# A hybrid decoder step on one core: loads and sums of the output projection in another order, more projection passes ahead of three places, the first memory-output products by heads, one table load per norm

## The chip, the cores and the metric

One core of a Trainium2 chip runs the whole step in one launch. The metric is the device time in microseconds (us). Before the change three runs gave 2590.53, 2591.98 and 2594.45 us, median 2591.98.

## What is computed

One decoder layer over 512 prompt tokens and 8 x 4 sample tokens (544 columns in all, width 2048): a mixer of two head groups, attention over a small memory, and a SwiGLU block, each behind an RMSNorm, in fp32.

```python
def decoder_layer(x, ...):
    y, ... = token_mixer(rmsnorm(x, norm_mix_w), ...)   # h @ w_in; 8 HGRN2 heads and 16 window heads; concat @ w_out
    x = x + y
    x = x + memory_attend(rmsnorm(x, norm_xattn_w), ...)  # q = h @ w_mq, softmax(q k) v, @ w_mo
    x = x + swiglu(rmsnorm(x, norm_ffn_w), ...)           # (silu(h @ w_gate) * (h @ w_up)) @ w_down
    return x, ...
...
def hgrn2_scan(q, k, g, v, s0):   # S_t = diag(exp g_t) S_{t-1} + k_t v_t^T, o_t = S_t^T q_t
```

## The kernel before, in words

All activations are held transposed, features on 128 partitions and tokens along the free dimension. A weight or an operand is split in two parts, hi (ScalarE, ACT) and lo (VectorE, DVE: the value minus hi); a product is three matmul passes, hi·hi, hi·lo, lo·hi, accumulated in PSUM. TensorE (PE) runs these passes from 60 us to the end, almost without a break. A tile framework schedules the program and fixes the order of instructions on each engine; each engine, and the queue of each engine that issues DMAs, works through its own list in order.

**HGRN heads** (250 to 790 us, `hgrn_head`, L910). Head h needs a chain of eight levels: PE forms `ha_ps` (L933) of qp and kp, DVE multiplies qp (L953) and kp (L956) by decays, and the next level's matmuls need these. Between the levels `draw(n)` (L355) takes n steps from the line of waiting matmul work, projection passes `in_ps` (L345) most of the time, so that PE has something to do. Ahead of level 0 stands `draw(8)` (L920). While head 0 runs, DVE and POOL (GpSimd) also prepare the window attention of the samples (`qbd` L771 and L786). While head 7 runs, the first unit of the output projection is being prepared already.

**Output projection** (786 to 974 us, `out_unit`, L1083). Eight units: two halves of the mixer's rows (r1 first, then r2) times four blocks of 512 output columns, in the order r1-0, r1-2, r1-3, r1-1, r2-2, r2-3, r2-0, r2-1. A unit multiplies a 1024 x 512 block of weights by a Strassen-like scheme in seven products, in the order B11, B21, T2, T1, T3, B22, T4. It loads four quarters A11, A21, A12, A22 (`oraw`, 512 KB each, issued on the SP queue, L1093). POOL forms S1 = A21 + A22, S2 = S1 - A11, S3 = A21 - A11 and later U = A12 - S2 (`ocomb`, L1099). The products take as weights, in their order: A11, A12, S2, S1, S3, U, A22. Each is split on ACT (`ohi` L1136, half by half `oh` L1137) and DVE (`olo` L1138) ahead of its 24 matmuls (`o_ps`, L1150); DVE adds the sums to x (L611). The operands B and T of a row group are made by `Rows` (L630 to L647): POOL forms sums of mixer outputs (`ot` L634, `mix` L635, L645, L647), ACT and DVE split them (`oB`, `oT`, L606 and L607). For r2 this work hangs in unit r1-1 as its hook: `rows2_parts` (L1241) is called after products 1 and 3. Units r2-3, r2-0 and r2-1 have a hook too, which splits and squares the finished rows of x for the next norm. For units r1-1 to r2-1 the quarter A22 comes from a pool wx with two buffers, the other three from a pool wr with four.

**Memory attention** (974 to 1076 us). `add_mq` (L1445) projects queries, `norm_rows` (L1232) makes 1/rms with Ln and Exp on ACT, one call of `rsqrt` (L80) per half of the columns, each with a load of the table set (L77). Then eight (head, half) units run: scores (`x_scores`, `xs_ps` L1465), softmax, transposes (`x_turn`, `xt_ps` L1476) and values (`x_values`, `xo_ps` L1487), with `draw` between them; the samples' part (`xso_ps` L1415, `xot_ps` L1425) is mixed in.

**Memory output** (1066 to 1140 us, `add_mo`, L1540). Product i takes the outputs of the four heads, `oxh`/`oxl`, as moving operand. The loop runs over the three passes outside and over the heads k inside, so that the last head is needed by the eighth matmul. `add_mo(0, 0)` and `add_mo(1, 0)` are queued right behind the last unit's values. After each product DVE adds to x (L1556) and, from the third on, ACT, DVE and POOL make the operands of the next block (`ffn_parts`, L1575).

**Feed-forward** (1136 to 2585 us): gate and up (`s_ps`, L1703; splits `shi` L1645, `h` L1646, `slo` L1647; POOL sums `scomb` L1665), then down. Their order is untouched but for the first gate unit, where the third `norm_rows` stands.

Of the kernel before, what the change touches and what calls it, by code (L numbers as in the profile page):

```python
# [19 lines left out]
P = 128  # L20
# [24 lines left out]
def hybrid_step(ctx: ExitStack, tc: tile.TileContext, a):  # L45
# [863 lines left out]
    def hgrn_head(h):  # L909
# [174 lines left out]
    def out_unit(rows, o4, old, hook=None):  # L1084

        n0 = o4 * 4 * P

        def load(f, c, last=False):
            p, n = (wx[0], 2) if rows2_on and last else (wr, 4)
            t = p.tile([P, WCH * P], F32, tag="raw", name="oraw", bufs=n)  # L1090
            t = t.rearrange("p (k c) -> p k c", k=DN)
            c0 = n0 + c * 2 * P
            dma(t, w_out[f * P : (f + DN) * P, c0 : c0 + 2 * P].rearrange("(k p) c -> p k c", p=P))  # L1093
            return t

        def comb(x, y, op):
            t = wst.tile([P, WCH * P], F32, tag="raw", name="ocomb", bufs=3)
            t = t.rearrange("p (k c) -> p k c", k=DN)
            nc.gpsimd.tensor_tensor(t, x, y, op)  # L1099
            return t  # L1100

        f0 = rows.g * 4
        A11, A21, A12, A22 = load(f0, 0), load(f0, 1), load(f0 + DN, 0), load(f0 + DN, 1, True)

        def run():
            S1 = comb(A21, A22, ALU.add)
            S2 = comb(S1, A11, SPLIT)
            S3 = comb(A21, A11, SPLIT)
            accs = [acc_tile("o_ps") for _ in range(2)]
            if next(units_made) % 2:  # L1110
                accs.reverse()
            o, x = (
                {
                    q: y[:, 2 * i : 2 * i + 2, t]
                    for q, (i, t) in dict(c11=(0, T0), c12=(0, T1), c21=(1, T0), c22=(1, T1)).items()
                }
                for y in (old, X[o4])
            )
            for i, (q, src, bank, first, dst, fresh) in enumerate((
                ("B11", A11, 0, True, "c11", True), ("B21", A12, 1, True, "c11", False),  # L1120
                ("T2", S2, 0, False, "c12", True), ("T1", S1, 1, True, "c22", True),
                ("T3", S3, 0, False, "c22", False), ("B22", None, 1, False, "c12", False),
                ("T4", A22, 0, False, "c21", True),
            )):
                rows.part(i)
                if src is None:
                    src = comb(A12, S2, SPLIT)
                hi = wst.tile([P, WCH * P], F32R, tag="hi", name="ohi")
                lo = wst.tile([P, WCH * P], F32R, tag="lo", name="olo")
                hi, lo = (t.rearrange("p (k c) -> p k c", k=DN) for t in (hi, lo))  # L1130
                if heads_done:
                    for j in range(2):
                        js = slice(2 * j, 2 * j + 2)
                        h2 = ps_to[0].tile([P, 2, 2 * P], F32R, tag="to"[j], name="oh2")
                        if j == 0:
                            nc.scalar.copy(hi, src)  # L1136
                        nc.scalar.copy(h2, src[:, js])  # L1137
                        nc.vector.tensor_tensor(lo[:, js], src[:, js], h2.bitcast(F32), SPLIT)  # L1138
                else:
                    split(hi, lo, src)  # L1140
                rows.part(i + 1)
                if hook:
                    hook(i)
                xh, xl = rows.ops[q]
                acc = accs[bank]
                for wt, xt_, at in ((hi, xh, 0), (hi, xl, 1), (lo, xh, 2)):
                    for p in range(2):
                        s = slice(p * P, (p + 1) * P)
# [78 lines left out]
    def norm_rows(out, sums, tag="t"):  # L1227

        for (b, e), s in zip(HALF, sums):
            pt = ps("nr_ps", tag)[:, : TT // 2]  # L1230
            n = s.shape[1]
            for u in range(n):  # L1232
                nc.tensor.matmul(pt, ones, s[:, u], start=u == 0, stop=u == n - 1)
            v = small.tile([P, TT], F32, tag="nv", name="nv", bufs=1)[:, : TT // 2]
            nc.vector.tensor_scalar(v, pt, 1.0 / D, EPS, ALU.mult, ALU.add)
            t = small.tile([P, TT], F32, tag="sqt", name="nt", bufs=2)[:, : TT // 2]
            rsqrt(out[:, b:e], v, t)

    rows2 = []

# [263 lines left out]
    for n, u in enumerate(units):  # L1504
        need(("mq", *u))
        if n:
            x_turn(*units[n - 1])
            draw(4)
        else:
            draw(36)  # L1510
        x_scores(*u)
        draw(14)
        if n:
            x_values(*units[n - 1])
        for _ in range(6 if n >= MH - 1 else 0):
            x_more(1)
            draw(5)
# [21 lines left out]
    def add_mo(i, half, done=None):  # L1539


        def run():
            if i not in mo_w:
                mo_w[i] = [next(wparts) for _ in range(MH)]
            acc = acc_tile("mo_ps")
            for at in range(3):
                for k, hi, lo in mo_w[i]:
                    wt, xt_ = (hi, hi, lo)[at], ox[half][k][at % 2]
                    for u in range(2):
                        nc.tensor.matmul(  # L1550
                            acc[:, u, :HT], wt[:, u * P : (u + 1) * P], xt_,
                            start=k + at == 0, stop=k == MH - 1 and at == 2,
                        )
                        yield
# [578 lines left out]
```

## Time and profile before

| | |
|---|---|
| median of three runs | 2591.98 us (2590.53 to 2594.45) |
| profiled execution | 2587.27 us, span 2585.5 us, mean granted clock 0.993 |
| PE busy | 2511.4 us, 97% of the span |
| DVE, ACT, POOL busy | 1708.9, 1557.7, 1104.3 us (66%, 60%, 43%) |
| DMA | 315.44 MB, 122 GB/s on average |

The profiled execution is the sum's base: 2587.27 us, of which 2585.5 are the span and 1.8 lie around it. It is 4.7 us under the median.

How to read it: PE is the engine that ends everything, so time is won or lost where PE waits. A row of PE's timeline shows in square brackets how long PE stood idle before the group and what ended that. PEclk in the windows view is the clock granted to TensorE as a share of 2.4 GHz (0.50 is 1.2 GHz).

### The profile page before, as it was taken

Reading aid. Unit: us, or ns where it says so; the run is one execution under the profiler, and the core shown is the slowest. Engines: PE = TensorE matmul, PEld = TensorE weight load, DVE = VectorE, ACT = ScalarE, POOL = GpSimd, SP = SyncE. Lnnn points to the kernel's source line nnn. Section 1 sums busy time; section 2 is a strip of 40 time slices with the busy share of each in tenths; the row PEclk is TensorE's granted clock in tenths of the full one; section 3 lists DMA queues with packets and bytes.
Section 4 is the critical chain, followed back from the end, with each engine's and each line's share of the span. In section 5 each row is a group of like instructions: output and inputs, shape, how many; then the busy total and the mean of one; then the engine's idle time right before and its main releaser. Section 6 shows DMA issues by size and latency. Waiting matters only on the chain.

```text
span 2585.5 us, 48037 instructions
## 1 busy us (share of the span) xinstructions
PE 2511.4 (97%) x19679; PEld 2443.3 (95%) x19679; DVE 1708.9 (66%) x2560; ACT 1557.7 (60%) x2181; POOL 1104.3 (43%) x643
## 2 busy tenths in 40 slices
PE   8999999999999999989999999999999999999997
PEld 7999999998998998779999999999999999999987
DVE  5555655565559796497666666666666676777887
ACT  5343223333327685467677777777776778767767
POOL 4101122122125631165555555555555566665752
PEclk9999999999999999999999999999999999999999
DMA  7222323554524226523333333333333453333325
GB/s 240 83 68 82 91 83 92 152 149 143 182 66 135 91 73 186 187 93 107 116 107 117 114 123 113 122 115 113 116 107 116 142 211 133 101 131 133 116 70 164
DMA packets 287164, 315.44 MB, mean 122 GB/s; under 512 B 9508, under 2 KB 239220, under 8 KB 284097
## 3 DMA queue, kind: packets, MB, share of 16 engines
q1 hardware_dynamic: 273024, 264.80, 32.2%
q0 software_dynamic: 13920, 47.58, 5.6%
q8 instruction: 155, 2.54, 0.4%
q14 instruction: 65, 0.52, 0.1%
HBM read 278.28 MB, written 33.64 MB: 121 GB/s over the span
## 4 chain that ended last, share of the span: by engine, by line
PE 54%; DVE 6%; ACT 3%; issue 2%; DMA 2%; POOL 1%; ACTq 0%; DVEq 0%; POOLq 0%; SPq 0%
PE s_ps L1703 48%; PE o_ps L1150 3%; PE d_ps L1987 1%; PE mq_ps L1445 1%; DVE slo L1647 1%; DMA wraw<-in_w_down_dram 1%; DVE wlo L132 1%; ACT shi L1645 0%; ACT h L1646 0%; DVE x L1887 0%; DMA xkv<-in_cache_mem_v_dram 0%; POOL scomb L1665 0%; DVE olo L1138 0%; DMA wraw<-in_w_mq_dram 0%; PE xk_ps L1363 0%
## 5 line engine op out<-in xcount | busy, mean ns | idle before, releaser
L1647 DVE TENSOR_TENSOR slo<-scomb,h 128x1024 fp32r<-128x1024 f32 x256 | 312.5, 1221 | 243.2 <-ACT h L1646 232.8
L1645 ACT CAST shi<-scomb 128x1024 fp32r<-128x1024 f32 x256 | 269.2, 1052 | 190.8 <-PE s_ps L1703 168.9
L131 ACT CAST whi<-wraw 128x1024 fp32r<-128x1024 f32 (+1 forms) x204 | 169.4, 845 | 342.0 <-PE in_ps L345 278.4
L1665 POOL TENSOR_TENSOR scomb<-sraw 128x1024 f32<-128x1024 f32 (+1 forms) x134 | 319.4, 2386 | 7.5 <-DVE slo L1647 2.5
L1665 POOL TENSOR_TENSOR scomb<-sraw,scomb 128x1024 f32<-128x1024 f32 (+1 forms) x67 | 166.5, 2486 | 327.9 <-DVE slo L1647 319.3
L1645 ACT CAST shi<-sraw 128x1024 fp32r<-128x1024 f32 x192 | 201.6, 1050 | 160.9 <-issue 99.5
L345 PE MATMUL in_ps<-xh,whi 128*128 128x272 f32 x1280 | 276.6, 297 | 0.8 <-ACT whi L131 0.8
L345 PE MATMUL in_ps<-xl,whi 128*128 128x272 f32 x1280 | 274.2, 295 | 0.0
L345 PE MATMUL in_ps<-xh,wlo 128*128 128x272 f32 x1280 | 272.1, 294 | 0.9 <-DVE wlo L132 0.8
L132 DVE TENSOR_TENSOR wlo<-wraw,whi 128x1024 fp32r<-128x1024 f32 (+1 forms) x204 | 208.0, 1033 | 96.6 <-ACT whi L131 92.1
L1646 ACT CAST h<-scomb 128x1024 fp32r<-128x1024 f32 x256 | 258.6, 1010 | 3.1 <-DVE slo L1647 3.0
L1647 DVE TENSOR_TENSOR slo<-sraw,h 128x1024 fp32r<-128x1024 f32 x192 | 233.8, 1218 | 28.0 <-ACT h L1646 23.2
L345 PEld LDWEIGHTS in_ps<-xh,whi 128*128 128x128 f32 x1280 | 201.8, 189 | 6.6 <-issue 4.3
L345 PEld LDWEIGHTS in_ps<-xh,wlo 128*128 128x128 f32 x1280 | 201.9, 189 | 6.4 <-issue 4.4
L345 PEld LDWEIGHTS in_ps<-xl,whi 128*128 128x128 f32 x1280 | 202.0, 189 | 5.1 <-issue 4.4
L1646 ACT CAST h<-sraw 128x1024 fp32r<-128x1024 f32 x192 | 194.1, 1011 | 17.8 <-DVE slo L1647 17.6
L1703 PE MATMUL s_ps<-T,shi 128*128 128x272 f32 x1408 | 191.9, 288 | 0.9 <-DVE T L607 0.5
L1703 PEld LDWEIGHTS s_ps<-T,shi 128*128 128x128 f32 x1408 | 182.8, 188 | 1.5 <-ACT T L606 0.8
L611 DVE TENSOR_TENSOR gu<-gu,s_ps 128x272 f32<-128x272 f32 x264 | 111.3, 435 | 109.4 <-PE s_ps L1703 106.8
L1703 PE MATMUL s_ps<-dT,shi 128*128 128x272 f32 x1280 | 173.8, 288 | 2.7 <-ACT h L1646 1.4
L1703 PEld LDWEIGHTS s_ps<-dT,shi 128*128 128x128 f32 x1280 | 165.1, 188 | 3.6 <-ACT h L1646 1.6
L1665 POOL TENSOR_TENSOR scomb<-scomb,sraw 128x1024 f32<-128x1024 f32 (+1 forms) x67 | 160.4, 2395 | 4.2
(523 smaller groups left out, 5723.6 us busy)
## 6 DMA issues: line engine op xcount, KB each, us to landing
sraw<-in_w_gate_dram SPq DMA_DIRECT2D x44, 1024.0 KB, 5.1
sraw<-in_w_up_dram SPq DMA_DIRECT2D x44, 1024.0 KB, 5.1
wraw<-in_w_in_dram SPq DMA_DIRECT2D x84, 512.0 KB, 4.0
sraw<-in_w_down_dram SPq DMA_DIRECT2D x40, 1024.0 KB, 5.2
oraw<-in_w_out_dram SPq DMA_DIRECT2D x32, 512.0 KB, 3.9
h_d<-gu POOLq DMA_DIRECT2D x22, 544.0 KB, 4.6
wraw<-in_w_mk_dram SPq DMA_DIRECT2D x16, 512.0 KB, 3.7
wraw<-in_w_mv_dram SPq DMA_DIRECT2D x16, 512.0 KB, 3.9
```

Source lines behind the costliest of these rows:

```text
L131: nc.scalar.copy(hi[:, s], raw[:, s])
L132: nc.vector.tensor_tensor(lo[:, s], raw[:, s], hi[:, s].bitcast(F32), SPLIT)
L345: nc.tensor.matmul(acc[:, i, : e - b], wt, xt[:, b:e], start=j + at == 0, stop=j == KD - 1 and at == 2,)
L611: nc.vector.tensor_tensor(out, x, y, ALU.add)
L1150: nc.tensor.matmul(acc[:, p, :HT], wt[:, k, s], xt_[:, k], start=first and k + at == 0, stop=k == DN - 1 and at == 2, skip_group_check=True,)
L1445: nc.tensor.matmul(acc, wt, xt_, start=j + at == 0, stop=j == KD - 1 and at == 2)
L1645: first = nc.scalar.copy(hi, src)
L1646: nc.scalar.copy(h2, src)
L1647: return first, nc.vector.tensor_tensor(lo, src, h2.bitcast(F32), SPLIT)
L1665: ins = nc.gpsimd.tensor_tensor(t[:, p], x[:, p], y[:, p], op)
L1703: nc.tensor.matmul(accs[p], wt[:, k, s], xt_[:, k], start=k + at == 0, stop=k == n - 1 and at == 2,)
L1987: nc.tensor.matmul(acc[:, 0, : e0 - b0], (hi, hi, lo)[at], hp[k][at % 2][:, b0:e0], start=k + at == 0, stop=k == nf - 1 and at == 2,)
```

## The change

Five edits. (1) In heads 0 and 7 the draw ahead of level 0 takes 16 steps instead of 8. (2) In units with a hook the loads are issued in the order A11, A21, A22, A12, all four from wr, and what the hook issues is ordered behind the unit's S3. (3) `norm_rows` loads the table set for the first half only. (4) The draw ahead of the first scores takes 47 steps instead of 36. (5) The first two memory-output products run head by head: all three passes of head 0, then of head 1, and so on.

```diff
@@ hgrn_head
-        draw(8)
+        draw(8 if 0 < h < H - 1 else 16)
@@ out_unit
             t = t.rearrange("p (k c) -> p k c", k=DN)
-            nc.gpsimd.tensor_tensor(t, x, y, op)
-            return t
+            return t, nc.gpsimd.tensor_tensor(t, x, y, op)
...
-        A11, A21, A12, A22 = load(f0, 0), load(f0, 1), load(f0 + DN, 0), load(f0 + DN, 1, True)
+        A11, A21 = load(f0, 0), load(f0, 1)
+        if hook:
+            A22 = load(f0 + DN, 1)
+            A12 = load(f0 + DN, 0)
+        else:
+            A12, A22 = load(f0 + DN, 0), load(f0 + DN, 1, True)
...
-            S3 = comb(A21, A11, SPLIT)
+            S3, summed = comb(A21, A11, SPLIT)
...
                 if hook:
-                    hook(i)
+                    with tc.issue_after(summed.ins):
+                        hook(i)
@@ norm_rows
-            rsqrt(out[:, b:e], v, t)
+            rsqrt(out[:, b:e], v, t, preload=b == 0)
@@ memory attention
-            draw(36)
+            draw(47)
@@ add_mo
-            for at in range(3):
-                for k, hi, lo in mo_w[i]:
-                    wt, xt_ = (hi, hi, lo)[at], ox[half][k][at % 2]
...
+            order = [(at, part) for at in range(3) for part in mo_w[i]]
+            if done is None and i < 2:
+                order.sort(key=lambda o: o[1][0])
+            for n, (at, (k, hi, lo)) in enumerate(order):
+                wt, xt_ = (hi, hi, lo)[at], ox[half][k][at % 2]
```

The numbers of instructions stay as they were, but for two table loads fewer on ACT. What moves shows at three places. (Line numbers of the changed kernel are up to seven higher.)

**The loads of unit r1-1 on the SP queue.** 9108, 9110, 9112 and 9114 are A11, A21 and the two others; the waits are semaphores of other engines and of DMA queues. Before:

```order
L1093 DMA oraw_9114<-in_w_out_dram 128x4x256 [waits DMASW5_49,DMASW4_49,DMASW6_49,DMASW2_49,DMASW7_49,DMASW1_49,DMAHW6_49,DVE_49,PE_49]
L1093 DMA oraw_9381<-in_w_out_dram 128x4x256
L1093 DMA oraw_8856<-in_w_out_dram 128x4x256 [waits DMAHW2_49,DVE_49]
L1093 DMA oraw_9108<-in_w_out_dram 128x4x256 [waits DMAHW3_49,DVE_49,Pool_49]
L1093 DMA oraw_9110<-in_w_out_dram 128x4x256 [waits DMAHW4_49]
L1093 DMA oraw_9112<-in_w_out_dram 128x4x256 [waits DMAHW5_49,Pool_49]
```

Now:

```order
L1093 DMA oraw_9381<-in_w_out_dram 128x4x256 [waits DMASW5_49,DMASW6_49,DMASW4_49,DMASW7_49,DMASW2_49,DMAHW6_49,DMASW1_49,PE_49]
L1093 DMA oraw_8856<-in_w_out_dram 128x4x256 [waits DMAHW2_49,DVE_49]
L1093 DMA oraw_9108<-in_w_out_dram 128x4x256 [waits DMAHW3_49,DVE_49,Pool_49]
L1093 DMA oraw_9110<-in_w_out_dram 128x4x256 [waits DMAHW4_49]
L1093 DMA oraw_9112<-in_w_out_dram 128x4x256 [waits DMAHW5_49,Pool_49]
L1093 DMA oraw_9114<-in_w_out_dram 128x4x256 [waits DMAHW1_49,Pool_49]
```

Before, 9114 is A22 and goes out ahead of the rest, and 9112 is A12. Now 9112 is A22 and 9114, the last, is A12, and 9114 waits for POOL: the program puts it into the buffer of 9110, this unit's A21, which S1 and S3 read. In r2-0 and r2-1 it is the same: the fourth load takes the buffer of the unit's own A21, the third that of the A12 that the unit before reads last in its U.

**POOL and ACT around unit r1-1.** 9036 is U of unit r1-3; 9116, 9118, 9120 and 9305 are S1, S2, S3 and U of r1-1. POOL now:

```order
L1099 TENSOR_TENSOR ocomb_9036<-oraw_8854,ocomb_8860 128x1024
L1099 TENSOR_TENSOR ocomb_9116<-oraw_9110,oraw_9112 128x1024
L1099 TENSOR_TENSOR ocomb_9118<-ocomb_9116,oraw_9108 128x1024
L1099 TENSOR_TENSOR ocomb_9120<-oraw_9110,oraw_9108 128x1024
L634 TENSOR_TENSOR ot1_9167<-mix0_406 128x1088
L635 TENSOR_TENSOR mix0_406<-mix0_406,mix1_407 128x4x272
L645 TENSOR_TENSOR mix0_406<-mix0_406 128x4x272
L647 TENSOR_TENSOR mix1_407<-mix1_407,mix0_406 128x4x272
L1099 TENSOR_TENSOR ocomb_9305<-oraw_9114,ocomb_9118 128x1024
```

ACT now, from B11's split (9124) to B21's (9158):

```order
L1141 CAST oh2_9126<-oraw_9108 128x512
L1140 CAST ohi_9124<-oraw_9108 128x1024
L1141 CAST oh2_9130<-oraw_9108 128x512
L606 CAST oT3_9508<-mix0_406 128x1088
L1141 CAST oh2_9160<-oraw_9114 128x512
L1140 CAST ohi_9158<-oraw_9114 128x1024
L1141 CAST oh2_9164<-oraw_9114 128x512
```

Before, L634, L635 and L645 stood on POOL ahead of the sums of unit r1-3, the unit before, and oT3's cast stood on ACT far ahead of r1-1; only L647 lay between S3 and U. Now all four lie between S3 and U, and oT3's cast, which reads what L635 writes, stands ahead of the cast of A12.

**PE at the end of the memory attention.** 10513, 10515, 10517 and 10519 are the hi parts of heads 0 to 3 (lo: one number higher). Before:

```order
L1550 MATMUL mo_ps<-oxh_10513,whi 128x272 x2
L1550 MATMUL mo_ps<-oxh_10515,whi 128x272 x2
L1550 MATMUL mo_ps<-oxh_10517,whi 128x272 x2
L1415 MATMUL xso_ps<-xkv,xpm 32x128 x8
L1425 MATMUL xot_ps<-ident,xos 128x128
L1476 MATMUL xt_ps<-ident,p 128x128 x4
L1487 MATMUL xo_ps<-pT,vm__10511 128x256 x2
L1550 MATMUL mo_ps<-oxh_10519,whi 128x272 x2
L1550 MATMUL mo_ps<-oxl_10514,whi 128x272 x2
```

Now, from xot on:

```order
L1430 MATMUL xot_ps<-ident,xos 128x128
L1557 MATMUL mo_ps<-oxh_10517,wlo 128x272 x2
L1557 MATMUL mo_ps<-oxh_10513,whi 128x272 x2
L1557 MATMUL mo_ps<-oxl_10514,whi 128x272 x2
L1557 MATMUL mo_ps<-oxh_10513,wlo 128x272 x2
L1557 MATMUL mo_ps<-oxh_10515,whi 128x272 x2
L1557 MATMUL mo_ps<-oxl_10516,whi 128x272 x2
L1557 MATMUL mo_ps<-oxh_10515,wlo 128x272 x2
L1557 MATMUL mo_ps<-oxh_10517,whi 128x272
L1481 MATMUL xt_ps<-ident,p 128x128 x4
L1557 MATMUL mo_ps<-oxh_10517,whi 128x272
L1557 MATMUL mo_ps<-oxl_10518,whi 128x272 x2
```

Ahead of the last head's values `xo_ps` stood 12 matmuls of the first two products before, and 36 of their 48 now; between `xot_ps` and `xt_ps` stood none, and 15 now; between `xt_ps` and `xo_ps` none, and 5 now.

## Rows read from the trace of the kernel before

**Rows 1.** the page, part 4: the chain that ended last, by engine

```profile
PE 54%; DVE 6%; ACT 3%; issue 2%; DMA 2%; POOL 1%; ACTq 0%; DVEq 0%; POOLq 0%; SPq 0%
```

**Rows 2.** waits view, PE: what for, us in total, times, longest

```profile
PE mo_ps L1550 <- DVE x L1556: 7.8, 5, 2.8
PE s_ps L1703 <- DVE slo L1647: 6.8, 7, 2.0
PE o_ps L1150 <- ACT ohi L1136: 3.7, 1, 3.7
PE ha_ps L933 <- DVE kp L956: 3.4, 2, 1.8
```

**Rows 3.** timeline, PE, 838 to 886: start, us, engine, line, operation

```profile
847.98 2.75 PE L1150 MATMUL o_ps<-oT,ohi 128*128 128x272 f32 x16 [3.69 <-ACT ohi L1136]
867.71 2.18 PE L1150 MATMUL o_ps<-oB,ohi 128*128 128x272 f32 x16
881.48 2.25 PE L1150 MATMUL o_ps<-oB,ohi 128*128 128x272 f32 x16 [1.53 <-DVE x L611]
```

**Rows 4.** timeline, POOL, 831 to 884

```profile
832.27 2.55 POOL L634 TENSOR_TENSOR ot<-mix 128x1088 f32<-128x1088 f32 x1
834.90 3.47 POOL L635 TENSOR_TENSOR mix<-mix,mix 128x1088 f32<-128x1088 f32 x1
841.96 2.47 POOL L1099 TENSOR_TENSOR ocomb<-oraw 128x1024 f32<-128x1024 f32 x1 [0.94 <-DMA oraw<-in_w_out_dram]
851.91 2.40 POOL L1099 TENSOR_TENSOR ocomb<-oraw,ocomb 128x1024 f32<-128x1024 f32 x1 [2.74 <-issue]
859.24 2.42 POOL L1099 TENSOR_TENSOR ocomb<-oraw 128x1024 f32<-128x1024 f32 x1
```

**Rows 5.** timeline, ACT, 832 to 885

```profile
866.30 0.59 ACT L1137 CAST oh<-ocomb 128x512 fp32r<-128x512 f32 x1 [0.82 <-DVE olo L1138]
866.96 1.05 ACT L1136 CAST ohi<-ocomb 128x1024 fp32r<-128x1024 f32 x1
868.43 1.10 ACT L606 CAST oB<-mix 128x1088 fp32r<-128x1088 f32 x1
```

**Rows 6.** DMA issues, windows 853 to 859 and 919 to 925: median us to landing last

```profile
oraw<-in_w_out_dram SPq DMA_DIRECT2D x1, 512.0 KB, 3.5
oraw<-in_w_out_dram SPq DMA_DIRECT2D x1, 512.0 KB, 3.9
```

**Rows 7.** windows view: us, busy times, PEclk, DMA share, GB/s

```profile
850.00:855.00 5.00, 5.00 (x31) 5.00 (x30) 3.69 (x6) 3.62 (x7) 3.01 (x2) 0.71 0.64 210
1074.00:1076.00 2.00, 1.57 (x4) 0.68 (x2) 0.00 (x0) 0.37 (x1) 0.00 (x0) 0.50 0.00 0
```

**Rows 8.** timeline, POOL then PE, 890 to 975

```profile
917.43 2.76 POOL L1099 TENSOR_TENSOR ocomb<-oraw,ocomb 128x1024 f32<-128x1024 f32 x1 [11.49 <-issue]
925.82 2.43 POOL L1099 TENSOR_TENSOR ocomb<-oraw 128x1024 f32<-128x1024 f32 x1
933.65 2.16 PE L1150 MATMUL o_ps<-oB,ohi 128*128 128x272 f32 x16
```

**Rows 9.** timeline, DVE then POOL, 750 to 790

```profile
755.79 2.59 DVE L956 TENSOR_TENSOR kp<-kp,tot 128x256 f32<-128x256 f32 x1
755.67 2.42 POOL L1099 TENSOR_TENSOR ocomb<-ocomb,oraw 128x1024 f32<-128x1024 f32 x1 [1.36 <-DVE wlo L132]
```

**Rows 10.** timeline, DVE, 248 to 272

```profile
258.78 2.67 DVE L786 COPY qbd<-sqs 64x64 f32<-64x64 f32 x2 [0.18 <-POOL qbd L771]
```

**Rows 11.** timeline, PE, 1050 to 1205

```profile
1071.68 1.09 PE L1476 MATMUL xt_ps<-ident,p 128*128 128x128 f32 x4 [1.92 <-DVE oxl L1339]
1076.03 0.82 PE L1550 MATMUL mo_ps<-oxh,whi 128*128 128x272 f32 x2 [0.46 <-ACT oxh L1338]
```

**Rows 12.** timeline, ACT, 982 to 996

```profile
984.82 1.28 ACT L77 ACT_TABLE_LOAD   x1
986.89 1.05 ACT L131 CAST whi<-wraw 128x1024 fp32r<-128x1024 f32 x1 [0.78 <-DMA wraw<-in_w_mq_dram]
```

More of the change, by code (lines that the diff above doesn't have):

```diff
@@ L1098, in comb @@
             t = t.rearrange("p (k c) -> p k c", k=DN)
-            nc.gpsimd.tensor_tensor(t, x, y, op)
-            return t
+            return t, nc.gpsimd.tensor_tensor(t, x, y, op)
         f0 = rows.g * 4
-        A11, A21, A12, A22 = load(f0, 0), load(f0, 1), load(f0 + DN, 0), load(f0 + DN, 1, True)
+        A11, A21 = load(f0, 0), load(f0, 1)
[4 more added lines that the diff above has]
+            A12, A22 = load(f0 + DN, 0), load(f0 + DN, 1, True)
         def run():
-            S1 = comb(A21, A22, ALU.add)
-            S2 = comb(S1, A11, SPLIT)
-            S3 = comb(A21, A11, SPLIT)
+            S1, _ = comb(A21, A22, ALU.add)
+            S2, _ = comb(S1, A11, SPLIT)
+            S3, summed = comb(A21, A11, SPLIT)
             accs = [acc_tile("o_ps") for _ in range(2)]
@@ L1126, in run @@
                 if src is None:
-                    src = comb(A12, S2, SPLIT)
+                    src, _ = comb(A12, S2, SPLIT)
                 hi = wst.tile([P, WCH * P], F32R, tag="hi", name="ohi")
@@ L1545, in run @@
             acc = acc_tile("mo_ps")
-            for at in range(3):
-                for k, hi, lo in mo_w[i]:
-                    wt, xt_ = (hi, hi, lo)[at], ox[half][k][at % 2]
[L1549 to L1554, printed above, removed]
+            order = [(at, part) for at in range(3) for part in mo_w[i]]
[3 more added lines that the diff above has]
+                wt, xt_ = (hi, hi, lo)[at], ox[half][k][at % 2]
+                for u in range(2):
+                    nc.tensor.matmul(
+                        acc[:, u, :HT], wt[:, u * P : (u + 1) * P], xt_,
+                        start=n == 0, stop=n == len(order) - 1,
+                    )
+                    yield
             x = X[i // 2][:, 2 * i % 4 : 2 * i % 4 + 2, (T0, T1)[half]]
```

## The prediction, made before the changed kernel ran

> **What bounds the kernel now.** I read the chain that ended last first: more than half of it is TensorE [rows 1], and PE is busy 97% of the span. So the change can only win or lose where PE stands still. Next I read the waits view for PE: its largest entries are a few microseconds in all and lie at the places that the diff touches [rows 2]. Then each place in the timelines: which wait ends last there, and what stands ahead of it on the engine that releases it. The granted clock comes last: after the 3.69 us wait of PE at 847.98 [rows 3] it is 0.71 of 2.4 GHz over the next five microseconds, and 0.50, the level of 1.2 GHz, at 1074, behind a cluster of waits [rows 7, 11]. A long wait costs more than its length.
>
> From the rows one number serves throughout. Seven products of 24 matmuls take 21 us when nothing waits, 3.02 us a product, 0.125 us a matmul.
>
> **The change part by part.**
>
> *Head 0, 16 more matmuls ahead of level 0 (draw counts pairs).* PE waits 1.6 us there now: of the two waits in the row of `ha_ps` the longest is 1.8 (head 7), the other is the rest of 3.4 [rows 2]. The order now puts DVE's eight `qbd` copies ahead of level 2's kp; they cannot begin before POOL's memset, at 258.78 [rows 10], and take some 3.4 us together. PE arrives 2.0 us later than before, kp of level 2 is ready some 4.9 us after 258.78 (the copies and three operations of half a microsecond), and my estimate is a wait of 2.1 instead of 1.6, and 0.5 more for the DMA that feeds b_ps, whose matmuls move a level forward. Term: +1.0. Bounds: -1.6 (the wait goes) and +2.5.
>
> *Head 7, the same.* DVE's kp took 2.59 us while POOL formed S2 of unit r1-0, from 755.67 to 758.09 [rows 9]; the wait of 1.8 is behind it. The extra work moves the weight splits of that stretch one level earlier, S2 with them: the wait moves from level 4 to level 3 and stays. S3 of the unit now meets kp of level 6, where the next level needs it, instead of the last level's: one more such wait, up to 1.8. And DVE has two more large splits ahead of the state S. Against it stand a wait before the head's norm and eight matmuls that are there earlier. Term: +1.5. Bounds: -1.5 (both collisions miss) and +4.
>
> *Unit r1-3.* Its T2 waits 3.69 us [rows 3], because S1 waits for A22, a DMA [rows 4]. That load waited for a DVE split that stood behind an operand split of r1-2, and went out beside two other loads. Now that split stands ahead, one load fewer is under way, and two POOL sums for r2 (at 832.27 and 834.90 [rows 4]) are no longer there. I take 2.8 us from waits, and with what is left short the clock row's loss goes too: 31 matmuls in five microseconds instead of some 42 [rows 7], 1.3 us. Term: -4.1. Bounds: -1 and -5.
>
> *Unit r1-1.* This is the largest loss. A12 is the weight of the second product. Count from the start of r1-3's U, 851.91, to the second product of r1-1, 867.71: 15.8 us [rows 3, 4]. Now A22 takes the buffer that this U reads, and A12 the buffer of the unit's own A21, which S3 reads last. U 2.4, the load of A22 3.5 [rows 6], S1 to S3 7.3 (3 x 2.42 [rows 4]), the load of A12 3.5: 16.7, then the cast 1.05 [rows 5], 17.8: 2.0 us late at the least. But ACT casts oT3 first, and that waits for two sums that now follow S3: 13.2 + 2.55 + 3.47 = 19.2 [rows 4], cast 1.10, half cast 0.59, cast 1.05 [rows 5]: 22, so 6.1 late. Queued behind that cast are all splits of the unit. POOL sums stretch where DVE reads beside them (3.47 beside 2.55), so up to 8. I take 5.5, and 1.3 for the clock, as after the wait of 3.69. Term: +6.8. The wait at 881.48 stays about as it is [rows 3].
>
> *Units r2-0 and r2-1.* No sums of a next group, but the same chain. From r2-3's U, 917.43, to B21 of r2-0, 933.65, are 16.2 us [rows 8]. The chain with each row's shorter value: 2.4 + 3.5 + 7.3 + 3.5 + 1.05 = 17.8, with the longer: 2.76 + 3.9 + 8.1 + 3.9 + 1.64 = 20.3 [rows 4 to 6, 8]. So 1.6 to 4.1 late; I take 2.75 twice. Term: +5.5. r2-3 follows a unit whose A22 came from wx, and its buffers are free early: nothing.
>
> *Start of the memory attention.* The draw of 47 changes nothing: the first scores stand at the same place in PE's order in both, since they wait for the second accumulator. The dropped table load ends at 986.10, and the next cast waits for its weights until 986.89 [rows 12]: cover 0.79 us, and without that DMA it would be worth at most 1.28. Term: 0, bounds -1.3 and +0.5.
>
> Of a switch of tables the Trainium skill (ScalarE: Activation LUTs, What ACT_TABLE_LOAD costs) says that a drain of about 1.38 us follows the load. The trace disagrees: the cast begins 0.79 us after the load ended. By the page the edit would free 2.66 us of ACT, part of which the DMA would not cover, and the sum would be some 1.9 lower; I keep to the row.
>
> *Memory output.* Between 1069.75 and 1076.03 PE does eight small matmuls and waits, for `xt_ps` 1.92 us and again behind it [rows 11]. Now 24 matmuls of the first two products fill it, 3.0 us, and eight that ran at half clock (0.50 [rows 7]) keep theirs: 1.0. Term: -4.0. Bounds: not more than -6 (the whole stretch and the clock), not less than -1: the next stop is DVE, which has the longest row of all waits behind it (`x`, 7.8 us [rows 2]); where it is the limit until 1140 the gain is given back.
>
> *First gate unit.* The second table load goes, and one `slo` moves ahead of the norm's arithmetic; the longest `slo` wait (2.0 [rows 2]) goes. PE then comes earlier to the next wait, which hangs on the norm's result, and that has not moved by as much. Term: -0.5. Bounds: -3 and +1.
>
> **The sum.** 1.0 + 1.5 - 4.1 + 6.8 + 5.5 + 0 - 4.0 - 0.5 = +6.2. On the profiled execution, 2587.3, that is 2593.5; on the median of the runs, 2592.0, it is 2598.2, which is the forecast. 0.2% is 5.2 us, about what a measurement of this kernel can tell from no change.
>
> **The rivals.**
>
> *A12 comes in time: faster.* Place: the second product of r1-1, r2-0, r2-1. Price: 12.3 us of the sum. It decides at 14.1 us after the U of the unit before: if A12 has landed by then, its two casts fit. That happens if U moves forward against PE (it waits for a buffer that DVE frees), or loads alone on the queues take 2 us less than the rows say. The sum is then -6.1, 2586. Against it: the loads of 3.5 and 3.9 are of just these tiles [rows 6], and S1 to S3 already follow each other without a break.
>
> *Same.* ACT's oT3 costs nothing (the sums follow S3 at once, the cast is covered) and r1-1 loses only 2.0, and the memory output gains its full 6: 6.2 - 4.8 - 2.0 = -0.6, 2591. For it: POOL's rows there are bounds, not measurements of the new order.
>
> *The regrouped memory products do not pay*, since DVE is the limit from 1080 to 1140: 6.2 + 4.0 = +10, 2602. For it: the row of `x` [rows 2]. It is in the slower part of the chances.
>
> *The change does not do what it says* for the draw of 47 and one of the table loads; that is in the sum, at nothing.
>
> **How the numbers follow.** The forecast with late A12 has 0.35, with the memory products not paying besides 0.11: slower 0.46. Same 0.25. A12 in time 0.29: faster. The range: the low end takes the rival's 2586 with the better bounds of the memory output and of head 0, 2581; the high end takes 2602 with r1-1 at its upper bound (2.5 more) and r2-0 and r2-1 at theirs (2.7 more), 2607. The forecast's own range is 2594 to 2606.
>
> **What would show it.** Right: in the changed profile PE waits for ACT `ohi` at the second product of r1-1 (4 to 8 us) and of r2-0 and r2-1 (1.6 to 4 us each), the SP queue's A12 goes out as S3 ends, and r1-3's T2 waits less than 2.5; between `xot_ps` and `mo_ps` the waits of 1.92 and 0.46 are under 1.5 in all. Wrong: no wait at those second products, or A12 out before S3's end; then the forecast falls with its largest term. If those waits are there and the time is still under 2587, the gains in the memory output or the heads are larger than the bounds here.

## The result, and the profile after

The changed kernel takes 2607.69 us (median of four runs, 2605.65 to 2611.59), the kernel before 2591.26 us beside it (four runs, 2586.95 to 2594.45). The ratio is 1.0066, 95% interval 1.0047 to 1.0085: 16.4 us slower. The prediction said slower by 6.2, 2598.2 us, between 2581 and 2607. The direction is right; the size is more than double, and lies just above the range.

The page, part 1, busy time by engine, and part 4, the chain that ended last:

```profile
PE 2521.2 (97%) x19679; PEld 2455.8 (94%) x19679; DVE 1703.2 (65%) x2560; ACT 1555.4 (60%) x2179; POOL 1100.6 (42%) x643
...
PE 54%; DVE 5%; POOL 2%; ACT 2%; issue 2%; DMA 2%; ACTq 0%; POOLq 0%; DVEq 0%
```

TensorE still bounds the kernel [rows 1]. Its busy time rose by 10 us with the same matmuls, so part of the loss is matmuls at half clock; the rest is waits. The waits view for PE says which (us in total, times, longest):

```profile
PE o_ps L1155 <- DVE x L611: 11.4, 4, 8.7
PE o_ps L1155 <- ACT ohi L1140: 9.8, 4, 2.8
PE mo_ps L1557 <- DVE x L1563: 8.1, 6, 2.9
PE s_ps L1710 <- DVE slo L1654: 3.5, 5, 1.2
PE ho_ps L1035 <- DVE S L1021: 3.3, 2, 3.1
```

Against the kernel before, `ohi` went from 3.7 us to 9.8 [rows 2]. Two rows have come up to the top: waits in the output projection released by DVE's add `x`, 2.9 us in all with none over 1.5 before, now with one of 8.7; and waits in head 7 released by DVE's copy of the state S, 0.2 us before, now with one of 3.1.

Where the time went is read by following one matmul through both traces: how much later it starts in the new one. Between two such matmuls the offset grows by what the stretch lost. The profiled run of before lies 4 us under its median, that of after 0.6 above, so the offsets end at 21.0 us, not 16.4; what kernels show that leave a place untouched must come off. The table has these offsets (us) for all kernels of the study, each from one profiled execution; the first column is the difference of the medians. Runs 1 to 11 are told below.

| kernel | time | end of head 6 to end of r1-2 | r1-3 | r1-1 | r2-0, r2-1 | memory output |
|---|---|---|---|---|---|---|
| the change | +16.4 | +8.3 | -3.2 | +10.7 | +8.8 | -4.4 |
| 1 loads alone | +12.3 | +1.3 | +1.1 | +3.2 | +7.8 | +0.1 |
| 2 order of sums alone | +2.9 | +1.2 | +2.0 | +5.2 | -0.1 | +0.1 |
| 3 heads 0 and 7 alone | +4.5 | +6.7 | +0.8 | 0 | -0.2 | +0.6 |
| 4 memory products alone | -6.6 | +1.3 | +1.1 | +0.1 | -0.2 | -5.1 |
| 5 A12 from wx | +5.2 | +8.0 | -0.6 | +8.8 | -0.1 | -4.9 |
| 6 head 7 back | +6.4 | +0.8 | -2.5 | +10.0 | +8.7 | -5.3 |
| 7 memory products, tables | -6.4 | +1.4 | +1.2 | 0 | 0 | -5.5 |
| 8 the same and head 0 | -11.2 | -0.2 | +0.7 | 0 | 0 | -5.1 |
| 9 oT3 behind | +6.8 | +8.0 | -4.4 | +4.5 | +7.1 | -4.9 |
| 10 its DVE part behind | +10.5 | +6.6 | -4.4 | +8.7 | +7.2 | -4.6 |
| 11 combined | -5.8 | -0.2 | -1.0 | +1.4 | -0.2 | -5.4 |

Kernels that leave head 7 alone show -0.2 to +1.4 in its column, those that leave r1-3 alone +0.7 to +1.2 in the next; the other columns are good to some tenths. So the change cost about 7.5 in head 7 and r1-2, gained 4.3 in r1-3, lost 10.7 and 8.8 in the three units with late A12, and gained 4.4 in the memory output and 0.7 at the first gate unit. That sums to 17.6, against 16.4 measured. Head 0 and the start of the memory attention come out at nothing.

**The second product of r1-1.** The timelines of the changed kernel (start, us, engine, line, operation, in brackets the idle time before and what ended it). PE, 851 to 884, where the first row answers to T2 and the next two to B21 of [rows 3]:

```profile
851.45 2.28 PE L1155 MATMUL o_ps<-oT,ohi 128*128 128x272 f32 x16 [2.83 <-ACT ohi L1140]
...
878.55 3.96 PE L1155 MATMUL o_ps<-oB,ohi 128*128 128x272 f32 x16 [8.71 <-DVE x L611]
882.31 1.97 PE L1155 MATMUL o_ps<-oB,olo 128*128 128x272 f32 x8
884.12 2.18 PE L1155 MATMUL o_ps<-oT,ohi 128*128 128x272 f32 x16
```

POOL, where U, S1 and S3 and then the two sums stand that [rows 4] showed ahead of r1-3:

```profile
855.62 2.41 POOL L1099 TENSOR_TENSOR ocomb<-oraw,ocomb 128x1024 f32<-128x1024 f32 x1 [2.97 <-issue]
861.79 2.41 POOL L1099 TENSOR_TENSOR ocomb<-oraw 128x1024 f32<-128x1024 f32 x1 [3.76 <-DMA oraw<-in_w_out_dram]
...
866.65 2.39 POOL L1099 TENSOR_TENSOR ocomb<-oraw 128x1024 f32<-128x1024 f32 x1
869.00 2.49 POOL L634 TENSOR_TENSOR ot<-mix 128x1088 f32<-128x1088 f32 x1
871.58 2.48 POOL L635 TENSOR_TENSOR mix<-mix,mix 128x1088 f32<-128x1088 f32 x1
```

ACT, then DVE, behind them:

```profile
874.09 1.10 ACT L606 CAST oT<-mix 128x1088 fp32r<-128x1088 f32 x1 [9.66 <-POOL mix L635]
875.09 0.58 ACT L1141 CAST oh<-oraw 128x512 fp32r<-128x512 f32 x1
875.61 1.04 ACT L1140 CAST ohi<-oraw 128x1024 fp32r<-128x1024 f32 x1
...
875.22 2.56 DVE L607 TENSOR_TENSOR oT<-mix,oT 128x1088 fp32r<-128x1088 f32 x1 [9.46 <-ACT oT L606]
877.70 0.70 DVE L611 TENSOR_TENSOR x<-x,o_ps 128x544 f32<-128x544 f32 x1
```

The chain is the forecast's up to ACT's cast: U (the first POOL row) ends at 858.03, A22 is issued at 858.05 and S1 starts 3.76 us after U; S3 ends at 869.04, A12 goes out at 869.06 and lands at 872.50, beside two loads for the next unit; ACT stands 9.66 us for oT3's source and has A12's cast ready at 876.65. But PE starts at 878.55. On DVE the low part of oT3 stands ahead of the add `x` of r1-3's last product, T4, and that add frees the accumulator of B21. DVE stood idle 9.46 us for ACT's oT3, then split it beside POOL's next sum (2.56 us), and only then added. After that B21's 24 matmuls take 5.57 us (878.55 to 884.12) instead of 3.02.

**Units r2-0 and r2-1.** Their second products answer to 933.65 in [rows 8]:

```profile
949.14 3.70 PE L1155 MATMUL o_ps<-oB,ohi 128*128 128x272 f32 x16 [2.62 <-ACT ohi L1140]
...
975.52 3.41 PE L1155 MATMUL o_ps<-oB,ohi 128*128 128x272 f32 x16 [2.22 <-ACT ohi L1140]
```

The windows view shows the clock (us, busy times, PEclk, DMA share, GB/s) around T2 of r1-3, at the second product of r1-1, and at those of r2-0 and r2-1:

```profile
850.00:855.00 5.00, 3.55 (x28) 3.55 (x29) 2.71 (x5) 4.35 (x7) 2.65 (x2) 1.00 0.23 67
...
878.00:884.00 6.00, 5.45 (x24) 5.48 (x25) 4.81 (x7) 4.96 (x7) 0.41 (x1) 0.50 0.00 0
949.00:954.00 5.00, 4.86 (x27) 4.86 (x28) 4.39 (x7) 5.00 (x10) 0.00 (x0) 0.66 0.15 51
975.50:980.50 5.00, 4.98 (x27) 4.99 (x28) 3.36 (x6) 5.00 (x9) 0.00 (x0) 0.66 0.00 0
```

The waits are a little under the forecast's 2.75 each, but the 24 matmuls behind them take 4.55 us (949.14 to 953.69) and 4.64 us (975.52 to 980.16) instead of 3.02.

**Head 7.** PE, DVE and POOL of the changed kernel, 751 to 781:

```profile
754.46 1.07 PE L933 MATMUL ha_ps<-qp,kp 128*128 128x64 f32 x8 [1.33 <-DVE kp L956]
766.24 1.08 PE L933 MATMUL ha_ps<-qp,kp 128*128 128x64 f32 x8 [1.68 <-DVE kp L956]
...
780.33 0.49 PE L1035 MATMUL ho_ps<-qp,S 128*128 128x128 f32 x2 [3.05 <-DVE S L1021]
...
763.49 2.60 DVE L956 TENSOR_TENSOR kp<-kp,tot 128x256 f32<-128x256 f32 x1
...
775.19 4.76 DVE L607 TENSOR_TENSOR oT<-mix,oT 128x1088 fp32r<-128x1088 f32 x1 [0.27 <-ACT oT L606]
779.98 0.29 DVE L1021 COPY S<-hk_ps 128x128 f32<-128x128 f32 x1
780.19 1.28 DVE L607 TENSOR_TENSOR oT<-ot,oT 128x1088 fp32r<-128x1088 f32 x1
...
763.32 2.49 POOL L1099 TENSOR_TENSOR ocomb<-oraw 128x1024 f32<-128x1024 f32 x1 [8.41 <-DVE wlo L132]
...
773.41 2.94 POOL L1007 TENSOR_TENSOR vm<-v,m 96x1024 fp32r<-96x1024 f32 x1
776.31 2.49 POOL L647 TENSOR_TENSOR mix<-mix,mix 128x1088 f32<-128x1088 f32 x1
```

Before there was one collision of kp with POOL, 2.59 us, and one wait behind it [rows 2, 9]. Now there are two, with waits of 1.33 and 1.68 us; and where the state S is wanted, DVE first splits a large operand. Alone that takes 1.28 us (780.19); beside POOL it took 4.76 and ended 1.15 us after POOL's second operation had ended, at 778.80. Copy S comes behind it, and PE waits 3.05 us. And the clock falls behind two of these three waits: it stays 1.00 over 754.46 to 757.46, but is 0.51 over 768 to 771 and 0.50 over 781.8 to 785. In r1-0 two more waits are new, 0.78 and 0.71 us for `olo` of DVE, and the 16 matmuls at 806.17 behind them took 3.45 us instead of 2.24.

The Trainium skill (SBUF — State Buffer, Who interferes with whom) says that a DVE instruction with two SBUF inputs contends with a GpSimd instruction that reads SBUF. The trace agrees: kp, which takes 0.42 us at other levels, took 2.60 us at 763.49 and ended 0.28 us after POOL's operation.

**Memory output.** PE between 1084 and 1101, against the waits of 1.92 and 0.46 in [rows 11]:

```profile
1091.96 0.65 PE L1420 MATMUL xso_ps<-xkv,xpm 128*32 128x128 f32 x16 [0.68 <-DMA xkv<-in_cache_mem_v_dram]
...
1098.29 0.77 PE L1557 MATMUL mo_ps<-oxh,whi 128*128 128x272 f32 x4 [0.46 <-ACT oxh L1343]
...
1100.38 1.27 PE L1557 MATMUL mo_ps<-oxh,whi 128*128 128x272 f32 x8 [0.31 <-DVE x L1563]
```

### The profile page after: what moved, and what is told of

Same layout as the page of the kernel before. It is cut to its first block, busy times and chain, and to the rows that moved or that the text cites. A ratio compares the mean times of both kernels' runs of the same rounds, so it can differ in the third digit from the quotient of the medians.

```text
span 2606.5 us, 48029 instructions
## 1 busy us (share of the span) xinstructions
PE 2521.2 (97%) x19679; PEld 2455.8 (94%) x19679; DVE 1703.2 (65%) x2560; ACT 1555.4 (60%) x2179; POOL 1100.6 (42%) x643
## 4 chain that ended last, share of the span: by engine, by line
PE 54%; DVE 5%; POOL 2%; ACT 2%; issue 2%; DMA 2%; ACTq 0%; POOLq 0%; DVEq 0%
PE s_ps L1710 47%; PE o_ps L1155 2%; PE mq_ps L1450 1%; PE d_ps L1994 1%; POOL ocomb L1099 1%; POOL scomb L1672 1%; DVE slo L1654 1%; DMA wraw<-in_w_down_dram 1%; DMA oraw<-in_w_out_dram 1%; DVE wlo L132 0%; DMA xkv<-in_cache_mem_v_dram 0%; ACT shi L1652 0%; DVE x L1894 0%; PE y_ps L1980 0%; ACT h L1653 0%
## 5 line engine op out<-in xcount | busy, mean ns | idle before, releaser
L1652 ACT CAST shi<-sraw 128x1024 fp32r<-128x1024 f32 x192 | 201.7, 1050 | 162.9 <-issue 99.7
```

The lines of the kernel that those rows point to most:

```text
L1652: first = nc.scalar.copy(hi, src)
```

## The experiments

The theory after the result: each part acts at its own place, and r1-1 loses more because oT3's split stands ahead of A12's cast on ACT and ahead of T4's add on DVE. The rivals: the late A12 alone; or the loads, by running beside others. "Before" is each time the kernel before on the same chip.

### 1. The loads alone

The kernel before, with the new order of loads in units with a hook:

```diff
-        A11, A21, A12, A22 = load(f0, 0), load(f0, 1), load(f0 + DN, 0), load(f0 + DN, 1, True)
+        A11, A21 = load(f0, 0), load(f0, 1)
+        if hook:
+            A22 = load(f0 + DN, 1)
+            A12 = load(f0 + DN, 0)
+        else:
+            A12, A22 = load(f0 + DN, 0), load(f0 + DN, 1, True)
```

> The kernel before with the load order of units with a hook alone (A11, A21, A22, A12, all from wr), the hook issued as before. If the late A12 is a cause by itself, PE waits for A12's cast at the second product of r1-1 by 2 to 3 us (the sums of the next rows are no longer in the way) and of r2-0 and r2-1 by 2 to 3 us each, with some clock loss: +6 to +10 us. If the loss of the change in r1-1 comes from the hook's order alone (the rival), r1-1 does not wait at its second product and the time is within 5 us of before or under it.

Measured: 2605.78 us (before 2593.48), ratio 1.0055 [1.0041, 1.0068], more than the 6 to 10 us expected. PE of this kernel, the second products of r1-1 and r2-0:

```profile
874.30 2.28 PE L1155 MATMUL o_ps<-oB,ohi 128*128 128x272 f32 x16 [1.54 <-ACT ohi L1141]
...
944.87 2.28 PE L1155 MATMUL o_ps<-oB,ohi 128*128 128x272 f32 x16 [2.93 <-ACT ohi L1141]
```

The late A12 costs 3.2 us in r1-1 and 7.8 in the two r2 units. Without the other order of sums r1-1 waits 1.54 us, less than the 2 to 3 expected and far less than 8.71, and r1-3 gains nothing: its T2 still waits 3.66. The rival falls: the late A12 costs by itself.

### 2. The order of the sums alone

```diff
                 if hook:
-                    hook(i)
+                    with tc.issue_after(summed.ins):
+                        hook(i)
```

> The kernel before with what the hook issues ordered behind S3, the loads as before. If oT3's split behind POOL's sums is a cause by itself, r1-1 waits 4 to 6 us at its first or second product, ended by ACT ohi or by DVE's add that frees the accumulator, with a clock loss of 1 to 3 behind it; r2-0 and r2-1 wait as little as before; r1-3's T2 waits less (-2 to -3): +2 to +6 us in all. If the loads alone are the cause (the rival), the only effect is r1-3's gain: -2 to -4 us.

Measured: 2596.39 us (before 2593.48), ratio 1.0008 [0.9999, 1.0016]; by place it loses 6 (0.9 in r1-3, 5.2 in r1-1), so how much it costs in all is uncertain. PE, T2 of r1-3 and the first product of r1-1:

```profile
847.91 4.00 PE L1150 MATMUL o_ps<-oT,ohi 128*128 128x272 f32 x16 [5.63 <-ACT ohi L1135]
...
869.21 2.28 PE L1150 MATMUL o_ps<-oB,ohi 128*128 128x272 f32 x16 [3.35 <-ACT ohi L1135]
```

Even with A12 there early, r1-1 loses 5.2 us: on ACT oT3's cast waits for its sum ahead of the first product's cast; the wait, 3.35 us, is under the 4 to 6 expected. And r1-3 does not gain, as both cases expected, but loses: its A22 goes out 2.4 us earlier than before but still runs beside r1-1's early load (7.1 us to landing), and lands at 841.90 where it landed at 841.89. So r1-3's gain in the change needs both edits: fewer loads at a time, and POOL free.

### 3. Heads 0 and 7 alone

```diff
-        draw(8)
+        draw(8 if 0 < h < H - 1 else 16)
```

> The kernel before with 16 steps instead of 8 ahead of level 0 in heads 0 and 7, nothing else. If the waits of head 7 come from these draws (two collisions of kp with POOL's sums and the state S behind a large split on DVE), the stretch from head 7 to unit r1-2 loses 6 to 9 us as in the changed kernel, and head 0 nothing: +6 to +9 us. If instead that stretch loses because later loads and sums moved (the rival), this kernel is within 3 us of before.

Measured: 2598.02 us (before 2593.48), ratio 1.0019 [1.0008, 1.003]. In head 7 the same three waits, 1.33, 1.68 and 3.05 us, to the hundredth; the last of them:

```profile
784.16 0.49 PE L1035 MATMUL ho_ps<-qp,S 128*128 128x128 f32 x2 [3.05 <-DVE S L1021]
```

The stretch loses 6.7 us, about 6 more than kernels that leave head 7 alone, at the low end of what was expected, and the rival falls; the time, +4.5, stays under the 6 to 9 expected. At head 0 the offset changes by no more than 0.6 us.

### 4. The memory products alone

```diff
-            for at in range(3):
-                for k, hi, lo in mo_w[i]:
-                    wt, xt_ = (hi, hi, lo)[at], ox[half][k][at % 2]
+            order = [(at, part) for at in range(3) for part in mo_w[i]]
+            if done is None and i < 2:
+                order.sort(key=lambda o: o[1][0])
```

> The kernel before with the first two memory-output products by heads, nothing else. If the waits between the last scores and the memory output go as in the changed kernel, -4 to -5 us and no wait over 0.6 us there but for a DMA. If DVE's work behind it takes the gain back (the rival), within 2 us of before, with larger waits for x between 1080 and 1140.

Measured: 2586.91 us (before 2593.48), ratio 0.9975 [0.9964, 0.9985], a little more gain than the 4 to 5 us expected. No wait between the last scores and the memory output is over 0.52 us. The largest wait for x between 1080 and 1140 grew, from 2.85 us to 3.87, but the gain is kept: the offset against before is +1.5 ahead of the memory output, -3.6 behind it and -3.5 still at 2000 us. The rival falls.

### 5. The change with A12 from the pool wx

```diff
         if hook:
             A22 = load(f0 + DN, 1)
-            A12 = load(f0 + DN, 0)
+            A12 = load(f0 + DN, 0, True)
```

> The changed kernel with A12 of units with a hook loaded into wx instead of wr; A22 stays in wr and everything else as changed, the orders of ACT and POOL in r1-1 too. A12 then waits for no sum of its own unit. Theory: r2-0 and r2-1 lose their waits at the second product (2.6 and 2.2 us and what hangs on them, together -8 us), while r1-1 keeps its wait within 1.5 us of 8.7, since there ACT's and DVE's oT3 behind POOL's L635 ends last: -7 to -9 us against the changed kernel, +6 to +10 against before. Rival: the late A12 ends the wait of r1-1 too, which then drops under 4 us, and the time comes within 4 us of before.

Measured: 2599.17 us (before 2593.94), ratio 1.0019 [1.001, 1.0028]. The waits of r2-0 and r2-1 are gone. A12 of r1-1 has now been in SBUF for some 30 us when it is wanted, and still, PE and then ACT at r1-1's second product:

```profile
885.73 3.96 PE L1155 MATMUL o_ps<-oB,ohi 128*128 128x272 f32 x16 [7.02 <-DVE x L611]
...
881.27 1.10 ACT L606 CAST oT<-mix 128x1088 fp32r<-128x1088 f32 x1 [7.92 <-POOL mix L635]
882.27 0.58 ACT L1141 CAST oh<-oraw 128x512 fp32r<-128x512 f32 x1
```

The wait is 1.7 us shorter than in the change, and the loss in time a little under the 6 to 10 expected. So in r1-1 the rival "the late A12 alone" falls: the wait hangs on oT3. In the r2 units, which have no such sums, the late load is all of it. Part of r1-3's gain goes, since A12 is again under way beside its A22.

### 6. The change with head 7 back at 8 steps

```diff
-        draw(8 if 0 < h < H - 1 else 16)
+        draw(16 if h == 0 else 8)
```

> The changed kernel with 8 steps ahead of level 0 in head 7 again (16 stay in head 0). Theory: the waits at level 3 and 6 and the one for S go, one of 1.8 at level 4 comes back, the stretch from head 7 to unit r1-2 is 5 to 8 us shorter, the waits of r1-1, r2-0 and r2-1 stay: +8 to +12 us against before. Rival: the waits in the units grow by what head 7 gives back, since the loads keep their distance to POOL's sums: within 3 us of the changed kernel, +14 to +18 against before.

Measured: 2600.35 us (before 2593.94), ratio 1.0029 [1.0016, 1.0041]: 10 us less than the change. Head 7 has one wait of 1.81 us again and no long one for S:

```profile
757.28 1.07 PE L933 MATMUL ha_ps<-qp,kp 128*128 128x64 f32 x8 [1.81 <-DVE kp L956]
```

The units r1-1 to r2-1 lose as in the change; the stretch from head 7 is 7.5 us shorter, as expected. The time, 6.4 us over before, is under the 8 to 12 expected. Copy S stands ahead of the large splits on DVE here.

### 7 and 8. The gaining parts

The kernel before with the memory products by heads and one table load per norm (7), and with 16 steps in head 0 besides (8); beside the diff of 4:

```diff
-            rsqrt(out[:, b:e], v, t)
+            rsqrt(out[:, b:e], v, t, preload=b == 0)
...
-        draw(8)
+        draw(16 if h == 0 else 8)
```

> The kernel before with the first two memory-output products by heads and one table load per norm, the two edits that gained in the changed kernel. Theory: -5 to -7 us, the memory output as in the run with it alone, and 0 to -1 us in the first gate unit. Rival: the table loads cost or gain more than 1 us beside it.

> The run before this with 16 steps in head 0 as well. Theory: head 0 loses one wait of 1.6 us and gains one of up to 1.5 for the relative-bias load: within 1.5 us of the run before. Rival: the wait behind the qbd copies grows, and it is 2 us or more slower.

Measured: 2587.59 us, ratio 0.9973 [0.9962, 0.9983], and 2582.76 us, ratio 0.9963 [0.995, 0.9975] (before 2593.94). Both beat both kernels. Run 8 lies 4.8 us under run 7, where 1.5 at most were expected; but the two intervals overlap, and the place of head 0 shows no gain, so what head 0 adds is not settled.

### 9 and 10. oT3's split behind T2's

In the changed kernel, the split of oT3 is ordered behind the splits of r1-1's third product, T2 (9), or its DVE part alone (10, without the first `issue_after`).

```diff
-            split(*self.ops[q], self.src[q])
+            if self.g == 0 and q == "T3":
+                with tc.issue_after(marks[-1][0].ins), tc.issue_after(marks[-1][1].ins):
+                    split(*self.ops[q], self.src[q])
+            else:
+                split(*self.ops[q], self.src[q])
...
+                    if rows.g == 2 and i == 2:
+                        marks.append((last_h, last_l))
```

> The changed kernel, with the split of oT3 (ACT's cast and DVE's low part) ordered behind the splits of r1-1's third product, T2; the loads stay as changed. Theory: in the changed kernel the wait of 8.71 us at r1-1's second product is set by oT3, not by A12, which had landed at 872.50. Without oT3 ahead, half cast 0.59 and cast 1.05 follow the landing: 874.1. PE has stood there since 869.84 (878.55 less 8.71), so 4.3 us are left, and with a shorter wait less of the 2.5 us at half clock: 4.4 to 6 us less than the changed kernel, 2602 to 2603.5 beside a kernel before of 2591 to 2594. Rival (the late A12 alone sets the wait): 8 to 9 us stay, and the time is within 2 us of the changed kernel's 2607.7. Rival 2 (oT3 only moves): r1-1 gains, but r2-2's fifth product or r1-1's T1 takes a new wait of 2 us or more.

> As the run before, but ACT's cast of oT3 stays ahead of A12's cast, and only DVE's low part of oT3 is ordered behind the splits of T2. Theory: r1-1's second product then starts after ACT's cast of A12, which ended at 876.65 in the changed kernel, instead of behind DVE's add that freed its accumulator at 878.40: wait 6.8 us instead of 8.71, released by ACT, about 2 us less than the changed kernel, 2604.5 to 2606.5. Rival (DVE's place in it is apparent only): 8.7 us stay, released by something else, and the time with it.

Measured: 2598.74 us, ratio 1.0028 [1.0017, 1.0039], and 2602.47 us, ratio 1.0039 [1.0024, 1.0054] (before 2591.93). PE at r1-1's second product and ACT ahead of it, in 9:

```profile
876.06 3.99 PE L1161 MATMUL o_ps<-oB,ohi 128*128 128x272 f32 x16 [3.97 <-ACT ohi L1144]
...
874.44 0.59 ACT L1145 CAST oh<-oraw 128x512 fp32r<-128x512 f32 x1 [7.76 <-DMA oraw<-in_w_out_dram]
```

and PE in 10:

```profile
874.52 3.56 PE L1161 MATMUL o_ps<-oB,ohi 128*128 128x272 f32 x16 [6.65 <-ACT ohi L1144]
```

The expected waits were 4.3 and 6.8. So, taken in this order, the 8.71 us come apart: 4.0 for the late load of A12, 2.7 more for oT3's cast on ACT, 2.1 more for its low part on DVE. The parts overlap, and the order matters: in run 5 oT3 alone, with A12 early, makes 7.02, to which the late load adds 1.7. The first rival of 9 falls, and so does the second: no new wait of 2 us comes later in r1-1 or r2-2. Both kernels fell further than these waits say, 5.9 us against the change in 10, where 2 were expected, and 9.6 in 9, where 4.4 to 6 were. At r1-1 itself the offset fell by 2.0 in 10 and 6.2 in 9; the rest lies in r1-0, r1-3 and the r2 units, which the edit does not touch and where the clock and the waits differ by one to two microseconds from kernel to kernel. In 10, for instance, the clock is 1.00 from 802 to 812 and from 970 to 980, where the change lost 1.2 us in r1-0 and 1.6 in r2-1 to half clock. Why they differ is open.

### 11. Combined

The change with the diffs of 5, 6 and 9, and the draw of 36 as before:

```diff
-            draw(47)
+            draw(36)
```

> The changed kernel with oT3's split behind T2's, A12 of units with a hook from the pool with two buffers, head 7 back to 8 steps, and the draw of 36 as before. Theory: head 7 at 0, r1-1 at 0 to +2 (A12 has landed early, oT3 no longer stands ahead), r2-0 and r2-1 at 0, memory output -4.4, first gate unit -0.7, and r1-3 between 0 and -2, since A12's early load runs beside its A22: 2583 to 2589, as the memory products by heads alone gave or a little better. Rival (A12's early load costs r1-3 more than the other order of sums gives): 2590 or more, with T2 of r1-3 waiting over 5 us.

Measured: 2586.17 us (before 2591.93), ratio 0.9975 [0.9966, 0.9985]. PE, T2 of r1-3 and the sixth product of r1-1:

```profile
845.54 3.59 PE L1161 MATMUL o_ps<-oT,ohi 128*128 128x272 f32 x16 [3.63 <-ACT ohi L1144]
...
879.20 3.15 PE L1161 MATMUL o_ps<-oB,ohi 128*128 128x272 f32 x16 [1.86 <-DVE x L611]
```

No second product waits, neither in r1-1 nor in the r2 units; r1-1's one wait stands at the sixth product, as in the kernel before (1.53 us [rows 3]). T2 of r1-3 waits as before. With all losses mended the other order of loads and sums gives nothing that 7 lacks. No run had early A12 and one load fewer at r1-3 at once; a fifth buffer in wr was not tried. The draw of 47 was never changed by itself.

## Why the prediction was right or wrong, point by point

**Direction and places: right.** The waits came where "what would show it" put them, released by ACT's `ohi` in the r2 units, with A12 going out 0.02 us after S3's end. The one in r1-1, 8.71 us, is longer than the 4 to 8 given, and DVE released it, not ACT. The rival "A12 comes in time" did not come; of its 14.1 us after U's start, A12 took 16.9 (855.62 to 872.50). By place the change lost 11.4 us more than the sum: 6.0 in head 7, 3.9 in r1-1 and 3.3 in the r2 units, less 1.8 elsewhere.

**Head 7, +1.5: the worst step.** It cost about 7.5, outside the bounds of -1.5 and +4. The step counted one more collision of kp with POOL, "up to 1.8", and got it. It saw that "DVE has two more large splits ahead of the state S" and gave them no price. The first of them made the 3.05 us wait, since it took 4.76 us beside two POOL operations; and the half clock behind the second and the third wait and in r1-0 was not counted either. Runs 3 and 6 show from both sides that the draw brings these waits.

**Unit r1-1, +6.8: 10.7.** The chain to ACT's cast was right, and its count, 6.1 us late, is close to the 6.65 that run 10 waits with DVE's part out of the way. But that closeness is partly luck. The chain took 21.0 us (855.62 to 876.65) instead of 22, since L635 took 2.48 us and not 3.47. And PE had 14.2 us (855.62 to 869.84) instead of the 15.8 counted, because T2 of r1-3 no longer ran at half clock: what the sum booked as a gain of the clock in r1-3 came back as waiting in r1-1. What failed is "queued behind that cast are all splits of the unit": the count stopped at ACT. The same operand's low part stands on DVE ahead of the add that frees the accumulator, 2.1 us more. And 1.3 for the clock was 2.55. Against this, "the wait at 881.48 stays" was wrong in the good direction: that wait of 1.53 us is gone.

**Units r2-0 and r2-1, +5.5: 8.8.** The waits, 2.62 and 2.22, were nearly right (2.75 taken). Left out were 1.5 and 1.6 us of half clock behind them, and a wait of 1.09 us in r2-0 that was 0.71 before.

**Unit r1-3, -4.1: -4.3.** Right in size, with another split: T2 still waits 2.83 us instead of 3.69, above the 2.5 given as a sign; another 0.9 us comes from a wait of 0.63 for `olo` at the end of r1-2 that went. The larger part is the clock, 1.00 after T2's wait instead of 0.71 [rows 7].

**Memory output, -4.0: -4.4,** in run 4 -5.1; the rival "the regrouped memory products do not pay" falls, since the gain outlasts the waits for DVE. **First gate unit, -0.5: -0.7.** The `slo` wait went, and another came (1.91 us at 1204.71), for an add on DVE that stands behind the norm's arithmetic. **Head 0, +1.0: about 0.** In the changed kernel its wait for kp went, and the one for b_ps grew from 0.30 to 1.50. **Start of the memory attention, 0: 0.** The table load that the change leaves at the first gate unit runs 1.28 us from 1189.25, and the next cast begins at 1190.55, so there too nothing follows the load that an engine would have to pay.

The likeliest case, at 0.35, was the one that came. But its range, 2594 to 2606, and the whole one had no term for the clock in head 7 and in the r2 units, and none for DVE's splits in head 7 and r1-1: these are the terms put at nothing that carried the time past the high end.

## What to carry to other kernels

When an operand's source is made later, follow every engine that splits it, not only the one that feeds the product: here DVE's half of one split, needed some 35 us later, held back the add that frees an accumulator. Price a moved DVE operation by what POOL does beside it, not by its own row. And look at a change's edits one at a time: of these five two lost, two did next to nothing (one of them, the draw of 47, only as far as the traces tell), and the one that gained was worth 5 us by its place.

## What the runs showed of the hardware

The length of a wait does not tell what the clock costs behind it. In the windows view the five microseconds behind a wait had these clocks: after 2.62 us 0.66 in the changed kernel, after 2.93 us 1.00 in run 1, after 3.35 us 1.00 and after 5.63 us 0.50 in run 2, after 3.97 us 0.52 in run 9, after 6.65 us 0.71 in run 10. Run 1, behind 944.87:

```profile
944.80:949.80 5.00, 4.93 (x39) 4.94 (x40) 4.46 (x7) 5.00 (x10) 0.00 (x0) 1.00 0.17 60
```

Run 9, behind 876.06:

```profile
876.00:881.00 5.00, 4.94 (x22) 4.94 (x23) 3.90 (x5) 5.00 (x9) 2.56 (x2) 0.52 0.18 62
```

The same 3.69 us of [rows 3] that the forecast took its 1.3 us from is thus no measure for other places: 16 matmuls behind a wait took 2.28 us at full clock and 2.75 to 4.0 otherwise, a difference of up to 1.7 us for the product's first part alone.

Part of the reason can be read from the rows: the clock can fall while PE still waits, and then part of the slow stretch is spent in the wait. In the changed kernel PE stands from 869.84 to 878.55, in run 10 from 867.87 to 874.52. The changed kernel, then run 10:

```profile
873.90:884.00 10.10, 5.45 (x24) 5.48 (x25) 7.60 (x8) 8.01 (x11) 3.06 (x3) 0.50 0.09 31
...
870.70:877.30 6.60, 2.77 (x12) 2.78 (x13) 2.92 (x5) 5.39 (x8) 3.67 (x2) 0.50 0.30 98
```

PE works 5.45 us of the first stretch at half clock and 2.77 us of the second. Why one wait is followed by such a stretch and another is not, no run here was made to find out.
